# Decay terms and mLSTM query and key projections issued in a written order, with the convolution's evacuation cut into four parts

## The chip, the cores and the metric

The kernel runs on one core of one Trainium2 chip. Five engines work side by side, each through its own instructions in order: TensorE (PE) multiplies matrices into PSUM, VectorE (DVE), ScalarE (ACT) and GpSimd (POOL) work on elements, SyncE (SP) issues most of the transfers. The metric is device time in microseconds (us) of one execution; the median of the runs counts.

## The reference

One layer of a bidirectional encoder over 272 positions (16 learned meta tokens and 256 inputs), width 2048, all in float32. The stretch of the program that the change touches computes this:

```
u = rmsnorm(h, norm1_g)                       # (272, 2048)
proj = u @ w_in                               # one projection, columns split up
m_qk = proj[:, :2048]; m_gates = proj[:, 4096:4112]
qk = silu(dwconv_centred(m_qk, conv_w))       # width 3: x[t-1]*w0 + x[t]*w1 + x[t+1]*w2
q, k = qk[:, :1024], qk[:, 1024:]             # 4 heads x 256
li = gates of input, lf = log_sigmoid(gates of forgetting), forwards and backwards
# mLSTM: scores q.k weighted with exp(cumsum(lf) - ... + li - running maximum),
# forwards and backwards, divided by max(|den|, exp(-m)), normalised per head
```

Behind it come differential attention, the gated merge of both branches, the output projection and a ConvGLU. Nothing of these is changed.

## The kernel before

**Tiling.** Every projection is a `gemm` over blocks of 256 weight columns. The weights stream in *pieces* of 128 x 1024 numbers, four pieces to a block over 2048 rows. A piece lands in `raw` (a transfer by SP), ACT casts it to `hi` (L157) and DVE forms `lo` = raw - hi (L115); PE then runs hi x hi, hi x lo and lo x hi, 24 products of 128 x 258 (or 272) to a piece, into two accumulators `acc` of PSUM, one for each 128 columns. Pieces are split three ahead of their use (`prepare`, `weights`); four `hi` and `lo` buffers, six `raw` buffers and three `acc` buffers limit how far ahead anything can run. Two more tiles of PSUM hold pairs (`two`), one is single (`one`).

**Evacuation.** At a block's last piece `evac(ci, a)` runs for each of its two accumulators. For queries and keys it is that of `conv_silu`: DVE multiplies the accumulator with the norm `rQ` or `rB` (L161; this frees the accumulator), ACT applies the middle tap (L456), DVE adds the other two taps (L457, L459), ACT applies Silu (L151) and casts, DVE subtracts (L115). `later` is a list of functions that `gemm` calls once after the products of the next piece (`flush`).

**The opening.** The first query block and the gates' products run inside `with in_order()`, so their instructions keep the program's order on every engine. From them come the norm factors `ss` (Ln and Exp on ACT, L151), three diagonal tiles `dg` (L419), their products with ones (L428), the norm `rB` (a copy by ACT, L429), and the gate values `gsb` (a multiplication on DVE, L161, and a bias on ACT, L472).

**Decay terms.** `decay_terms` is a generator. It spreads `gsb` over partitions by eight small products (L483, L484; two tiles `two`), copies them out, forms log_sigmoid and runs scans and differences on DVE (L492 to L528) that fill `rows` and `acol`; two transposes (L533) end it. `weave(front, back)` takes one step of the generator `front`, then one piece of `back`, until `front` is done.

**What sets the order.** Outside `in_order()` a list scheduler of the framework picks, engine by engine, what stands next in each row of instructions; the engines keep to that row. Between the opening and the end of the program only activations are tied to each other: `activation` keeps functions of one table together, since a change of table costs an instruction of its own.

**Behind the stretch.** `values` projects the values while `heads1` makes the scores of four heads; then `heads2` (inside `weave` with the second branch's query projection `roped`) inverts the denominators, spreads them (`spread`), weighs the scores of a head (`merged`, into the single buffer `hl`), multiplies with the values (`outputs`: products `two<-hl`, then a square on ACT, L710, a cast, L711, and a subtraction on POOL, L712) and normalises (`normed`: products `one<-t` with ones).

Of the kernel before, what the change touches and what calls it, by code (L numbers as in the profile page):

```python
# [12 lines left out]
AF = mybir.ActivationFunctionType  # L13
# [51 lines left out]
def hybrid_layer(ctx, tc, x, meta, norm1_g, w_in, conv_w, gate_bias, mnorm_g, lq1, lk1, lq2, lk2,  # L65
# [23 lines left out]
    def unit(shape, dtype=F32):  # L89
        return units.tile([P] + shape, dtype, tag="u", name="u")  # L90
# [5 lines left out]
    def r1(n=NT, dtype=F32):  # L96
        return tmp.tile([P, n], dtype, tag="r1", name="r1")
# [16 lines left out]
    def low(out, src, hi):  # L114
        V.tensor_tensor(out=out, in0=src, in1=hi.bitcast(F32), op=ALU.subtract)  # L115

    @contextmanager
    def in_order():

        traced = nc.cur_bb.bb.instructions  # L120
        start, last = len(traced), {}
        yield
        for i in traced[start:]:
            if i.engine in last:
                behind(i, last[i.engine])
            last[i.engine] = i
# [8 lines left out]
    def activation(out, in_, func, **kw):  # L135

        k = KIND[func]
        if k != table[0]:
            before, since[:] = since[:], []
            table[0] = k  # L140
            if k == 0:
                first = S.preload_act_table_set("natural_log_exp_and_others").ins
                for i in before:
                    behind(first, i)
                before = [first]
                since.append(first)
            a = S.activation(out, in_, func, **kw)
            for j in before:
                behind(a.ins, j)
        else:  # L150
            a = S.activation(out, in_, func, **kw)  # L151
            behind(a.ins, since[0])
        since.append(a.ins)
        return a

    def split(hi, lo, src):
        S.copy(hi, src)  # L157
        low(lo, src, hi)

    def mul(o, a, b, eng=V):  # L160
        eng.tensor_tensor(out=o, in0=a, in1=b, op=ALU.mult)  # L161
# [98 lines left out]
    def weave(front, back):  # L260
        for _ in front:
            next(back, None)
        run(back)
# [184 lines left out]
    def conv_silu(dst, f, r, nt):  # L448
        hi, lo = pair(nt)
        dst.append((hi, lo))  # L450

        def evac(ci, a):
            j = f + ci
            u, c = r1(nt), r1(nt)
            mul(u, a, r)
            S.activation(c, u, AF.Copy, scale=cw(1, j))  # L456
            V.scalar_tensor_tensor(out=c[:, 1:nt], in0=u[:, 0:nt - 1], scalar=cw(0, j), in1=c[:, 1:nt],  # L457
                                   op0=ALU.mult, op1=ALU.add)
            V.scalar_tensor_tensor(out=c[:, 0:nt - 1], in0=u[:, 1:nt], scalar=cw(2, j), in1=c[:, 0:nt - 1],  # L459
                                   op0=ALU.mult, op1=ALU.add)  # L460
            activation(c, c, AF.Silu)
            split(hi[:, ci, :], lo[:, ci, :], c)
        return evac

    put = conv_silu(qs, 0, rQ, NT)
# [13 lines left out]
    def decay_terms():  # L479

        pli, plf = two(), two()
        for d in range(2):
            PE.matmul(pli[:, d, :L], sel[0:32, d * P:(d + 1) * P], gsb[0:32], start=True, stop=True)  # L483
            PE.matmul(plf[:, d, :L], sel[0:32, (2 + d) * P:(3 + d) * P], gsb[0:32], start=True, stop=True)  # L484
        li, lf, e, y, w = (unit([2, L]) for _ in range(5))
        S.copy(lf, plf[:, :, :L])
        S.copy(li, pli[:, :, :L])

        S.activation(e, lf, AF.Abs)
        activation(e, e, AF.Exp, scale=-1.0)  # L490
        yield
        V.tensor_scalar(out=y, in0=e, scalar1=1.0, scalar2=None, op0=ALU.add)  # L492
        V.tensor_scalar(out=w, in0=y, scalar1=1.0, scalar2=None, op0=ALU.subtract)
        V.tensor_tensor(out=e, in0=e, in1=w, op=ALU.subtract)
        activation(y, y, AF.Ln)
        activation(w, y, AF.Exp, scale=-1.0)
        yield
        mul(e, e, w)
        yield
        add(e, e, y)  # L500
        yield
        V.scalar_tensor_tensor(out=lf, in0=lf, scalar=0.0, in1=e, op0=ALU.min, op1=ALU.subtract)
        yield

        V.tensor_tensor_scan(out=m[:, 0, :], data0=lf[:, 0, :], data1=li[:, 0, :], initial=0.0, op0=ALU.add, op1=ALU.max)
        V.tensor_tensor_scan(out=m[:, 1, ::-1], data0=lf[:, 1, ::-1], data1=li[:, 1, ::-1], initial=0.0,
                             op0=ALU.add, op1=ALU.max)
        yield

        V.memset(rows[:, 258:260], 0.0)  # L510
        zero = unit([L])
        V.memset(zero, 0.0)
        acol = unit([2, L])
        for si, (s0, n) in enumerate(ST):
            cum = r1(L)
            V.tensor_tensor_scan(out=cum[:, s0:L], data0=lf[:, 0, s0:L], data1=zero[:, s0:L], initial=0.0,
                                 op0=ALU.add, op1=ALU.add)
            lo_t, at = max(s0, T0), (F0c, F1c, F2c)[si]
            V.tensor_tensor(out=rows[:, at:at + L - lo_t], in0=cum[:, lo_t:L], in1=m[:, 0, lo_t:L], op=ALU.subtract)
            V.tensor_tensor(out=acol[:, 0, s0:s0 + n], in0=li[:, 0, s0:s0 + n], in1=cum[:, s0:s0 + n], op=ALU.subtract)  # L520
            yield
            cum = r1(L)
            end, lo_c, at = s0 + n, min(s0, T0), (B0c, B1c, B2c)[si]
            rev = lambda a: a[:, lo_c:end][:, ::-1]
            V.tensor_tensor_scan(out=rev(cum), data0=rev(lf[:, 1, :]), data1=rev(zero), initial=0.0,
                                 op0=ALU.add, op1=ALU.add)
            V.tensor_tensor(out=rows[:, at:at + end - T0], in0=cum[:, T0:end], in1=m[:, 1, T0:end], op=ALU.subtract)
            V.tensor_tensor(out=acol[:, 1, s0:end], in0=li[:, 1, s0:end], in1=cum[:, s0:end], op=ALU.subtract)  # L528
            yield
        for d in range(2):  # L530
            pt = one()
            for si, (s0, n) in enumerate(ST):
                PE.transpose(pt[0:n, si * P:(si + 1) * P], acol[:, d, s0:s0 + n], ident)  # L533
            ptv = pt[:, 0:384].rearrange("p (s h q) -> p s h q", s=3, q=32)
            V.tensor_copy(aT[0:16, d, 0, :], ptv[0:16, 0, :, 0])
            V.tensor_copy(aT[:, d, 1:3, :], ptv[:, 1:3, :, 0])
            yield

    def keys():
        for b in range(4):  # L540
            yield from gemm(w_in, 16, K0 + 256 * b, 256, us, 0, L, conv_silu(ks, 8 + 2 * b, rB, L))

    def queries():
        for b in range(1, 4):
            yield from gemm(w_in, 16, Q0 + 256 * b, 256, us, T0, NT, conv_silu(qs, 2 * b, rQ, NT))

    weave(decay_terms(), chain(queries(), keys()))


    def values(c0, centred):  # L550
# [578 lines left out]
```

## Time and profile before

| | |
|---|---|
| median of 3 runs | 1569.02 us (1568.3 to 1572.68) |
| the profiled execution | 1567.98 us, of which the span of its instructions 1565.9 us |
| PE busy with products | 1542.8 us, 99% of the span |
| DVE, ACT, POOL busy | 66%, 49%, 5% |
| the chain that ended last | 95% PE, 2% DVE, 1% ACT |

PE's share is nearly the whole span, so the table says only that time lies where PE does not run, or runs at the lower of its two clocks; where that is, the rows below show.

### The profile page before, as it was taken

How to read it: one execution, taken by the hardware profiler on the slowest of the kernel's cores; microseconds unless marked ns; L12 is line 12 of the kernel's file. 1: busy time of each engine (PE TensorE's matmuls, PEld its weight loads, DVE VectorE, ACT ScalarE, POOL GpSimd, SP SyncE). 2: the span in 40 equal slices, each digit the busy share in tenths (PEclk: the TensorE clock that was granted, in tenths of full speed). 3: DMA queues.
4: the chain of work that ended last, by engine and by line, in shares of the span. 5: the costliest groups of instructions: out<-in, count | busy, mean ns of one | idle time of the engine just before them, and what ended most of it. 6: DMA issues, size and time to landing. Idle time of an engine off the chain costs nothing.

```text
span 1565.9 us, 28925 instructions
## 1 busy us (share of the span) xinstructions
PE 1542.8 (99%) x11825; PEld 1491.2 (95%) x11825; DVE 1028.8 (66%) x1617; ACT 763.7 (49%) x1147; POOL 81.0 (5%) x120
## 2 busy tenths in 40 slices
PE   8899989999999999999999999999999999999997
PEld 8899989999999999999999999999888999999887
DVE  6786688758886545665666676666444676766544
ACT  5656445444655433554555444444333454545443
POOL 1130113100000000000110000000000000000000
PEclk9999999999999999999999999999999999999999
DMA  9365425654456655555555555555555655655552
GB/s 262 108 202 161 149 82 166 188 167 131 124 174 201 188 177 188 185 180 182 195 167 182 187 183 188 181 183 178 198 189 188 188 176 188 187 179 186 184 193 95
DMA packets 255097, 274.52 MB, mean 175 GB/s; under 512 B 11460, under 2 KB 232773, under 8 KB 254949
## 3 DMA queue, kind: packets, MB, share of 16 engines
q1 hardware_dynamic: 251378, 269.01, 54.1%
q10 hardware_dynamic: 3587, 3.68, 0.8%
q8 instruction: 92, 1.51, 0.4%
q14 instruction: 40, 0.33, 0.1%
HBM read 270.55 MB, written 2.10 MB: 174 GB/s over the span
## 4 chain that ended last, share of the span: by engine, by line
PE 95%; DVE 2%; ACT 1%; issue 1%; POOL 0%; DMA 0%; SPq 0%; DVEq 0%; POOLq 0%; ACTq 0%
PE acc L172 90%; PE two L172 2%; DVE lo L115 1%; PE two L846 1%; PE one L172 0%; PE one L858 0%; PE two L568 0%; POOL t L712 0%; ACT hi L157 0%; PE two L977 0%; PE two L965 0%; DMA r<-in_norm_g_dram 0%; DVE u L730 0%; DVE u L115 0%; POOL t L164 0%
## 5 line engine op out<-in xcount | busy, mean ns | idle before, releaser
L172 PE MATMUL acc<-u,hi 128*128 128x258 f32 (+1 forms) x6592 | 1201.8, 285 | 4.9 <-DVE r L161 4.9
L172 PEld LDWEIGHTS acc<-u,hi 128*128 128x128 f32 x6592 | 1018.3, 189 | 7.2 <-DVE r L161 5.1
L172 PE MATMUL acc<-u,lo 128*128 128x258 f32 (+1 forms) x3296 | 924.0, 284 | 0.7 <-DVE lo L115 0.7
L115 DVE TENSOR_TENSOR lo<-raw,hi 128x1024 fp32r<-128x1024 f32 (+1 forms) x500 | 616.8, 1234 | 422.5 <-ACT hi L157 420.6
L157 ACT CAST hi<-raw 128x1024 fp32r<-128x1024 f32 (+1 forms) x500 | 523.3, 1048 | 648.4 <-PE acc L172 504.4
L172 PEld LDWEIGHTS acc<-u,lo 128*128 128x128 f32 x3296 | 621.3, 190 | 1.9 <-DVE lo L115 1.2
L172 PE MATMUL acc<-hi,u 128*128 128x512 f32 (+1 forms) x704 | 209.5, 381 | 0.0
L172 PEld LDWEIGHTS acc<-hi,u 128*128 128x128 f32 x704 | 130.6, 189 | 26.3
L172 PE MATMUL acc<-lo,u 128*128 128x512 f32 (+1 forms) x352 | 134.8, 383 | 0.0
L172 PEld LDWEIGHTS acc<-lo,u 128*128 128x128 f32 x352 | 66.2, 188 | 13.7
L161 DVE TENSOR_TENSOR r<-acc,r 128x258 f32<-128x258 f32 x88 | 37.3, 424 | 12.4 <-PE acc L172 12.4
L115 DVE TENSOR_TENSOR u<-r,u 128x256 fp32r<-128x256 f32 (+2 forms) x93 | 37.7, 436 | 4.9 <-ACT u L157 4.4
L1025 ACT ACTIVATE r<-r,fcT 128x256 f32<-128x256 f32 x88 | 39.9, 501 | 0.0
L157 ACT CAST u<-r 128x256 fp32r<-128x256 f32 (+2 forms) x93 | 34.6, 405 | 9.7 <-DVE r L161 7.0
L1026 DVE SCALAR_TENSOR_TENSOR r<-r,fcT,r 128x256 f32<-128x256 f32 x88 | 38.5, 479 | 0.0
L1027 DVE SCALAR_TENSOR_TENSOR r<-r,fcT,r 128x255 f32<-128x255 f32 x88 | 38.4, 479 | 0.0
L151 ACT ACTIVATE r<-r 128x256 f32<-128x256 f32 (+2 forms) x77 | 29.6, 412 | 3.5 <-DVE r L459 3.1
L161 DVE TENSOR_TENSOR r<-r,r 128x256 f32<-128x256 f32 (+1 forms) x57 | 22.1, 419 | 0.1
L161 DVE TENSOR_TENSOR r<-acc,u 128x258 f32<-128x258 f32 x32 | 13.5, 422 | 12.9 <-PE acc L172 12.9
L161 DVE TENSOR_TENSOR r<-acc,rB 128x272 f32<-128x272 f32 (+1 forms) x38 | 16.1, 429 | 4.8 <-PE acc L172 4.7
L164 DVE TENSOR_TENSOR u<-acc,u 128x512 f32<-128x512 f32 (+1 forms) x18 | 10.6, 625 | 12.7 <-PE acc L172 12.7
L151 ACT ACTIVATE t<-two,sm 128x272 f32<-128x272 f32 x32 | 15.3, 482 | 5.5 <-DVE sm L802 5.5
(241 smaller groups left out, 754.3 us busy)
## 6 DMA issues: line engine op xcount, KB each, us to landing
raw<-in_w_up_dram SPq DMA_DIRECT2D x176, 512.0 KB, 4.2
raw<-in_w_in_dram SPq DMA_DIRECT2D x175, 512.0 KB, 3.5
raw<-in_w_down_dram SPq DMA_DIRECT2D x88, 512.0 KB, 3.7
raw<-in_w_out_dram SPq DMA_DIRECT2D x32, 512.0 KB, 3.3
raw<-in_w_branch_m_dram SPq DMA_DIRECT2D x16, 512.0 KB, 3.3
raw<-in_w_branch_d_dram SPq DMA_DIRECT2D x16, 512.0 KB, 3.3
t<-in_x_dram ACTq DMA_DIRECT2D x8, 256.0 KB, 3.4
out_dram<-u SPq DMA_DIRECT2D x8, 256.0 KB, 2.8
```

The source lines that it names most:

```text
L115: V.tensor_tensor(out=out, in0=src, in1=hi.bitcast(F32), op=ALU.subtract)
L151: a = S.activation(out, in_, func, **kw)
L157: S.copy(hi, src)
L161: eng.tensor_tensor(out=o, in0=a, in1=b, op=ALU.mult)
L164: eng.tensor_tensor(out=o, in0=a, in1=b, op=ALU.add)
L172: PE.matmul(o, p, q, start=first and i == 0, stop=last and i == len(ops) - 1)
L846: PE.matmul(ps[:, i, 0:L], dq[h // 2][p][o:o + 64, h % 2, 2 + P * qt:2 + P * (qt + 1)], dk[h // 2][q][o:o + 64, h % 2, :], start=(p, q) == ...
L1025: S.activation(z, u[:, 2:NT], AF.Copy, scale=fcT[:, 1, f:f + 1])
L1026: V.scalar_tensor_tensor(out=z, in0=u[:, 1:NT - 1], scalar=fcT[:, 0, f:f + 1], in1=z, op0=ALU.mult, op1=ALU.add)
L1027: V.scalar_tensor_tensor(out=z[:, 0:SEQ - 1], in0=u[:, 3:NT], scalar=fcT[:, 2, f:f + 1], in1=z[:, 0:SEQ - 1], op0=ALU.mult, op1=ALU.add)
```

## The change

Two things change. `weave(decay_terms(), chain(queries(), keys()))` now stands inside `with in_order()`, so on each engine its instructions follow each other as the program writes them. And `evac` of `conv_silu` only multiplies the accumulators with the norm; the taps, Silu with its cast, and the subtraction follow in three functions that `later` calls after the first, second and third piece of the next block. `decay_terms` has three more yields, ahead of and behind its two copies out of PSUM.

```diff
--- before.py
+++ after.py
@@ -449,17 +449,33 @@
         hi, lo = pair(nt)
         dst.append((hi, lo))
 
+        uc = []
+
+        def taps():
+            for ci, (u, c) in enumerate(uc):
+                S.activation(c, u, AF.Copy, scale=cw(1, f + ci))
+            for ci, (u, c) in enumerate(uc):
+                V.scalar_tensor_tensor(out=c[:, 1:nt], in0=u[:, 0:nt - 1], scalar=cw(0, f + ci), in1=c[:, 1:nt],
+                                       op0=ALU.mult, op1=ALU.add)
+                V.scalar_tensor_tensor(out=c[:, 0:nt - 1], in0=u[:, 1:nt], scalar=cw(2, f + ci), in1=c[:, 0:nt - 1],
+                                       op0=ALU.mult, op1=ALU.add)
+            later.append(silu)
+
+        def silu():
+            for ci, (_, c) in enumerate(uc):
+                activation(c, c, AF.Silu)
+                S.copy(hi[:, ci, :], c)
+            later.append(rest)
+
+        def rest():
+            for ci, (_, c) in enumerate(uc):
+                low(lo[:, ci, :], c, hi[:, ci, :])
+
         def evac(ci, a):
-            j = f + ci
-            u, c = r1(nt), r1(nt)
-            mul(u, a, r)
-            S.activation(c, u, AF.Copy, scale=cw(1, j))
-            V.scalar_tensor_tensor(out=c[:, 1:nt], in0=u[:, 0:nt - 1], scalar=cw(0, j), in1=c[:, 1:nt],
-                                   op0=ALU.mult, op1=ALU.add)
-            V.scalar_tensor_tensor(out=c[:, 0:nt - 1], in0=u[:, 1:nt], scalar=cw(2, j), in1=c[:, 0:nt - 1],
-                                   op0=ALU.mult, op1=ALU.add)
-            activation(c, c, AF.Silu)
-            split(hi[:, ci, :], lo[:, ci, :], c)
+            uc.append((r1(nt), r1(nt)))
+            mul(uc[ci][0], a, r)
+            if ci == 1:
+                later.append(taps)
         return evac
 
     put = conv_silu(qs, 0, rQ, NT)
@@ -483,8 +499,11 @@
             PE.matmul(pli[:, d, :L], sel[0:32, d * P:(d + 1) * P], gsb[0:32], start=True, stop=True)
             PE.matmul(plf[:, d, :L], sel[0:32, (2 + d) * P:(3 + d) * P], gsb[0:32], start=True, stop=True)
         li, lf, e, y, w = (unit([2, L]) for _ in range(5))
+        yield
         S.copy(lf, plf[:, :, :L])
         S.copy(li, pli[:, :, :L])
+        yield
+        yield
 
         S.activation(e, lf, AF.Abs)
         activation(e, e, AF.Exp, scale=-1.0)
@@ -544,7 +563,8 @@
         for b in range(1, 4):
             yield from gemm(w_in, 16, Q0 + 256 * b, 256, us, T0, NT, conv_silu(qs, 2 * b, rQ, NT))
 
-    weave(decay_terms(), chain(queries(), keys()))
+    with in_order():
+        weave(decay_terms(), chain(queries(), keys()))
 
 
     def values(c0, centred):
```

Lines behind the change are numbered some 20 higher in it (L483 becomes L499, L457 becomes L458). The rows of instructions of the built programs differ from the opening to the end of `heads2`; behind that they are the same.

**PE, end of the opening.** `one<-r` are the products with the diagonal tiles (L428), L434 turns the parameters, L499 and L500 are the gates' products of `decay_terms`, `acc` the first streamed block. Rows of before have -, of the change +; those with a blank are in both.

```order
-L172 MATMUL acc<-u,lo 128x258
-L172 MATMUL acc<-u,hi 128x258
 L428 MATMUL one<-r_489,ones 128x16
 L428 MATMUL one<-r_490,ones 128x128
 L428 MATMUL one<-r_491,ones 128x128
+L434 MATMUL one<-ident,r_126 128x105
+L499 MATMUL two<-r_522,t_135 128x272
+L500 MATMUL two<-r_522,t_135 128x272
+L499 MATMUL two<-r_522,t_135 128x272
+L500 MATMUL two<-r_522,t_135 128x272
+L172 MATMUL acc<-u,hi 128x258 x2
+L172 MATMUL acc<-u,lo 128x258
```

Before, 73 streamed products stand between the last products of the opening and L428, and more ahead of the gates' products; now none does, and the first streamed product stands behind L500.

**DVE, the second streamed block's accumulators and the decay terms.** Before (`r_839` and `r_848` are the two products of an accumulator with the norm, L505 to L525 scans, L519 to L528 differences of the decay terms):

```order
L505 SCALAR_TENSOR_TENSOR u<-u 128x272
L506 SCALAR_TENSOR_TENSOR u<-u 128x272
L512 MEMSET u 128x272
L516 SCALAR_TENSOR_TENSOR r_771<-u 128x272
L525 SCALAR_TENSOR_TENSOR r_805<-u 128x16
L161 TENSOR_TENSOR r_839<-acc,rB 128x258
L519 TENSOR_TENSOR rows<-r_771,u 128x258
L520 TENSOR_TENSOR u<-u,r_771 128x16
L527 TENSOR_TENSOR rows<-r_805,u 128x2
L528 TENSOR_TENSOR u<-u,r_805 128x16
L161 TENSOR_TENSOR r_848<-acc,rB 128x258
```

In the change (`r_825` and `r_828` are the same two, L524 and L525 the first two scans):

```order
L521 SCALAR_TENSOR_TENSOR u<-u 128x544
L115 TENSOR_TENSOR lo<-raw,hi 128x1024
L161 TENSOR_TENSOR r_825<-acc,rB 128x258
L161 TENSOR_TENSOR r_828<-acc,rB 128x258
L524 SCALAR_TENSOR_TENSOR u<-u 128x272
L525 SCALAR_TENSOR_TENSOR u<-u 128x272
L115 TENSOR_TENSOR lo<-raw,hi 128x1024
L458 SCALAR_TENSOR_TENSOR r_826<-r_825,prmT,r_826 128x257
L460 SCALAR_TENSOR_TENSOR r_826<-r_825,prmT,r_826 128x257
L458 SCALAR_TENSOR_TENSOR r_829<-r_828,prmT,r_829 128x257
```

The two multiplications have moved ahead of the scans, and directly behind the split (`lo`) of a later piece.

**PE, heads 0 and 1 of `heads2`.** Before (`t_2598` and `t_2599` are the squares of head 0, `two<-hl` the products of head 1 that follow):

```order
L172 MATMUL acc<-u,lo 128x258
L172 MATMUL acc<-u,hi 128x258 x2
L172 MATMUL one<-t_2599,ones 128x258
L172 MATMUL one<-t_2598,ones 128x258
L172 MATMUL one<-t_2599,ones 128x258
L172 MATMUL acc<-u,lo 128x258
L172 MATMUL two<-hl,v_1597 128x258 x2
L172 MATMUL two<-hl,v_1598 128x258
L172 MATMUL two<-hl,u 128x258 x6
```

In the change (`t_2599` and `t_2600` are the squares of head 0, `t_2792` and `t_2793` those of head 1):

```order
L172 MATMUL two<-hl,u 128x258 x6
L172 MATMUL two<-hl,v_1585 128x258
L172 MATMUL one<-t_2599,ones 128x258
L172 MATMUL two<-hl,v_1585 128x258
L172 MATMUL two<-hl,v_1586 128x258
L172 MATMUL two<-hl,u 128x258 x6
L172 MATMUL two<-hl,v_1585 128x258 x2
L172 MATMUL two<-hl,v_1586 128x258
L172 MATMUL two<-hl,u 128x258 x6
L172 MATMUL one<-t_2600,ones 128x258
L172 MATMUL one<-t_2599,ones 128x258
L172 MATMUL one<-t_2792,ones 128x258
```

Before, 39 streamed products stand between the products of head 0 and the last ones on its squares, and the products of the two heads are apart; now the products of head 0, of head 1, and those on the squares of both heads stand next to each other without a streamed product.

## Rows read from the trace of the kernel before

**Rows 1.** Waits of PE over the whole span: total us, times, longest

```profile
PE acc L172 <- DVE r L161: 4.9, 1, 4.9
PE two L172 <- issue: 2.8, 1, 2.8
...
PE two L172 <- DVE u L723: 1.0, 1, 1.0
PE acc L172 <- DVE lo L115: 0.7, 2, 0.5
PE one L172 <- POOL t L712: 0.5, 1, 0.5
...
PE two L172 <- DVE u L115: 0.3, 1, 0.3
```

**Rows 2.** Timeline of PE, end of the opening: start us, us

```profile
27.95 4.14 PE L172 MATMUL two<-u 128*32 128x272 f32 x32
...
40.29 1.03 PE L428 MATMUL one<-r,ones 16*128 16x16 f32 x6
...
50.01 0.72 PE L483 MATMUL two<-r,t 32*128 32x272 f32 x2
...
52.04 0.39 PE L172 MATMUL acc<-u,lo 128*128 128x258 f32 x1
```

**Rows 3.** Timeline of ACT, the norm and the gate bias

```profile
35.32 0.30 ACT L151 ACTIVATE sm<-sm,eps 128x3 f32<-128x3 f32 x1 [1.47 <-DVE sm L415]
...
36.46 0.20 ACT L151 ACTIVATE sm<-sm 128x3 f32<-128x3 f32 x1
...
41.36 0.39 ACT L429 COPY rB<-one 128x272 f32<-128x272 f32 x1 [0.15 <-PE one L428]
...
46.76 0.52 ACT L472 ACTIVATE r<-r,gb 32x272 f32<-32x272 f32 x1 [0.88 <-DVE r L161]
```

**Rows 4.** Timeline of DVE, the norm and an accumulator's release

```profile
37.73 0.15 DVE L332 SCALAR_TENSOR_TENSOR sm<-sm 128x3 f32<-128x3 f32 x1
...
38.39 0.61 DVE L419 TENSOR_SCALAR r<-ident,sm 16x16 f32<-16x16 f32 x3
...
68.08 0.40 DVE L161 TENSOR_TENSOR r<-acc,rB 128x258 f32<-128x258 f32 x1
```

**Rows 5.** The chain that ended last: start us, us, what

```profile
68.54 5.00 PE acc L172 x23
...
491.58 231.18 PE acc L172 x1926
```

**Rows 6.** Stretches of 1 us: length, busy us of PE to POOL, granted clock, DMA

```profile
69.00:70.00 1.00, 1.00 (x7) 1.00 (x7) 1.00 (x4) 0.55 (x2) 0.00 (x0) 0.50 0.00 0
...
210.00:211.00 1.00, 1.00 (x7) 1.00 (x7) 1.00 (x6) 0.43 (x1) 0.57 (x1) 0.50 0.00 0
```

**Rows 7.** The page's costliest groups: a split; its mean in ns is second

```profile
L115 DVE TENSOR_TENSOR lo<-raw,hi 128x1024 fp32r<-128x1024 f32 (+1 forms) x500 | 616.8, 1234 | 422.5 <-ACT hi L157 420.6
```

**Rows 8.** Timeline of DVE beside POOL's broadcast of `rows`

```profile
75.67 2.18 DVE L115 TENSOR_TENSOR lo<-raw,hi 128x1024 fp32r<-128x1024 f32 x1
```

**Rows 9.** Timeline of POOL, the broadcast itself

```profile
74.30 6.07 POOL L606 PARTITION_BROADCAST FB<-rows  x4 [30.46 <-PE acc L172]
```

**Rows 10.** Timeline of PE: the last sums of `heads1`, the first `spread` of `heads2`

```profile
201.25 0.52 PE L172 MATMUL two<-t,selr 128*128 128x258 f32 x3
...
207.60 0.35 PE L172 MATMUL two<-u 128*128 128x258 f32 x1 [2.83 <-issue]
```

**Rows 11.** Timeline of ACT behind the products of head 0

```profile
219.83 0.60 ACT L710 ACTIVATE t<-two 128x516 f32<-128x516 f32 x1 [2.07 <-PE two L172]
220.46 0.62 ACT L711 CAST t<-t 128x516 fp32r<-128x516 f32 x1
220.99 0.84 ACT L157 CAST hl<-FB 128x774 fp32r<-128x774 f32 x1
```

**Rows 12.** Timeline of DVE and POOL behind the products of head 0

```profile
221.23 1.31 POOL L712 TENSOR_TENSOR t<-t,t 128x516 fp32r<-128x516 f32 x1 [10.65 <-ACT t L711]
222.71 0.96 DVE L115 TENSOR_TENSOR hl<-FB,hl 128x774 fp32r<-128x774 f32 x1
```

## The prediction

> **What bounds the kernel now.** The page comes first: PE is busy for 99% of the span and the chain that ended last lies on PE for 95%, so a change here counts by what PE waits for, or by the clock it runs at. The second view is the list of all that PE waited for [rows 1]: the reader is to see that one wait of 4.9 us stands out, for an accumulator that DVE had not released, and that four of 2.8, 1.0, 0.5 and 0.3 us (4.6 together) belong to one later place, `heads2`. A list of the same kind by stretches has nothing between these two places and nothing from there to the tail. The third view is the timeline of each engine at these places.
>
> A wait has a second price, which only the chain and the granted clock show. Behind the wait of 4.9 us, 23 streamed products take 5.00 us [rows 5]; at the rate of the long stretch (231.18 us for 1926, 0.120 us each [rows 5]) they would take 2.76. The granted clock there is 0.50 [rows 6], the lower level, 1.2 GHz. So this wait cost 4.9 + 2.2 = 7.1 us. The places in `heads2` also fell to 0.50 for a time [rows 6].
>
> **What the change does to the long wait.** Before, DVE's row holds the release of the second block's accumulators behind a chain of decay terms; the first release came at 68.08 [rows 4], and PE began at 68.54 [rows 5]. In the new row both releases stand ahead of the scans and need only what PE itself finishes. I count the whole 7.1 us as gone.
>
> **What the written order adds at the opening.** Before, PE fills the time in which the norm is worked out with 73 streamed products; now the gates' products must come first, and they need the norm. Step by step, from before's rows:
> - The opening's last 32 products began at 27.95 and took 4.14 us [rows 2]. The four streamed products ahead of them (0.5 us) are gone too, so PE is through at about 31.4.
> - Ln begins at 35.32 (0.30) and Exp takes 0.20 [rows 3]. Before, a cast and a split of the next pieces stood in between; the new rows of ACT and DVE don't hold them there, so Exp ends at 35.9. The three small DVE operations up to the diagonals take 0.66 (37.73 to 38.39 [rows 4]): the diagonals begin at 36.5 and end at 37.1. Nothing in the change can make PE's next product begin earlier.
> - The products with the diagonals take 1.03 [rows 2] and end near 37.6; the copy of `rB` (0.39 [rows 3]) ends at 38.0; three multiplications on DVE (0.40 for one [rows 4], which start 0.35 apart) end at 39.2; the gate bias (0.52 [rows 3]) ends at 39.7.
> - So the gates' products begin at 39.8, not 50.01 [rows 2], and the first streamed product comes behind them. They take 2.03 (50.01 to 52.04 [rows 2]), as before.
>
> Between 31.4 and 39.8 PE has 1.3 us of work (1.03 and one transpose): it waits 7.1 us. Since 4.9 us brought the clock down before, I take the same 2.2 us for the clock, and 0.4 for the products of the chain itself, which then run at half rate: 9.7 us. The bounds: 7.1 if the clock never falls, 12 if it stays down twice as long.
>
> What waits here on ACT and DVE costs nothing by itself: the first block's four pieces are split by then, and the fifth needs a buffer that PE frees.
>
> **What it adds in the query blocks.** DVE's work for a block is four splits of 1.23 [rows 7], two releases, four taps and two subtractions of about 0.4, some 7.7 us of the 11.5 us that PE takes for 96 products. The decay terms are 10.2 us of DVE, by my count of their rows at the spacing of the trace. Both stay the same, but before much of it ran while PE had 73 products to do; now it falls on four blocks: 4 x 7.7 + 10.2 = 41 of 46 us. DVE just keeps up, but any release that stands behind a split [the second excerpt of the change] comes late, since an accumulator is wanted half a piece after a block begins. I walked the rows: block by block, such waits come at the third query block (0.4 us), the first key block (0.8) and the second (1.3), where POOL's broadcast falls. Together 2.5; before, two waits for splits were 0.7 [rows 1], so +1.8. Bounds: 0, and 5 us, one split of 1.23 late in each of four blocks.
>
> The four parts of the evacuation bring no new work: the same operations in the same number. Two more table changes come, because the last key block's Silu now runs among the exponentials of `heads1`; ACT is free half of its time there, and the splits that queue behind them are wanted some 2 us later. I cost them at nothing; without that cover a late split would stop PE for what it is late, at most the 12 exponentials between them (an estimate, at the 0.4 us of other ACT rows of this size: some 5 us).
>
> **What it adds in `heads2`.** This is not written by the change; the scheduler placed it anew.
> - The reciprocal: from the end of the last sums (201.77) to the first `spread` (207.60) [rows 10] the chain takes 5.8 us. Before, 25 products (3.0 us) covered it and 2.8 were waited. Now 40 do (4.8): 1.0 is left. Behind it two short waits for splits, 0.8 together.
> - Heads 0 and 1: `hl` is one buffer, so head 1's products need head 0's to be through, then ACT's square and cast, and DVE's subtraction. In rows: the cast of `hl` begins 0.5 us behind the square's cast, and the new order has it directly behind the square, ending 1.5 us behind head 0's last product; DVE's part of 0.96 [rows 12] ends at 2.5. Head 1's products run to 4.6. Then its square (0.60 [rows 11]), another cast of `hl` (0.84), a Ln and its own cast (0.62) end near 6.9, and POOL's subtraction (1.31 [rows 12]) at 8.2. In these 8.2 us PE has 24 products (2.9 us): it waits 5.4, where before streamed products filled most of it.
>
> Together 1.0 + 0.8 + 5.4 = 7.2 against 4.6 [rows 1]: +2.6. The clock falls before and, I think, after; I take that as even. Bounds: -6 (no wait, no fall) and +6 (as counted, with another 2.2 for the clock, and POOL slower).
>
> **The sum.** 9.7 - 7.1 + 1.8 + 2.6 = +7.0 us. Against the profiled execution's own 1567.98 us (span 1565.9) that is 1575.0. The median of the runs, 1569.02, is 1.0 above this execution; the forecast for the median is 1576.
>
> **One rule beside a row.** While POOL broadcasts `rows` (6.07 us [rows 9]) a split takes 2.18 us [rows 8] instead of 1.23 [rows 7]: 0.95 more. In the change `rows` is complete some 10 us later, in the first key block, where DVE has no slack left. I carry 0.95 once, inside the 1.3. The Trainium skill, page "SBUF — State Buffer", section "Who interferes with whom", says that a DVE instruction with two SBUF inputs contends with a GpSimd instruction that reads SBUF, and that the second to issue is fully blocked for the whole instruction. The trace bears it out for single splits. By that rule all of the broadcast's 6.07 us may be lost to DVE.
>
> **Rivals.**
> 1. *DVE becomes the bound.* If the broadcast holds DVE for all its 6.07 us and not for one split's 0.95, the splits of the second key block are late by 5.1 more. For it: 41 of 46 us. Against it: before, the two splits beside the broadcast held PE only 0.7 us in all. PE would wait 5 us more: 1581. It decides when DVE's slack (5 us in four blocks) is used up ahead of the broadcast.
> 2. *Waits change places.* The written order's 9.7 replaces 7.1, the query blocks add nothing beyond the 0.7 of before, `heads2` comes out even: +2.6, 1571.5. For it: before's list shows no other wait in 100 us of key and value blocks. Against it: the rows of `heads2` in the change.
> 3. *Not slower.* `heads2` sets the sign. If head 1's chain is covered after all, because PE comes late to these rows and finds ACT, DVE and POOL done, then its 4.6 us and its clock loss of about 2 go, and the longer cover of the reciprocal does the rest: 9.7 - 7.1 + 1.8 - 6.6 = -2.2, 1567. It decides where the casts of `hl` and the squares end ahead of PE, some 5 us earlier than I count. Against it: they need PE's own products.
> 4. *Nothing changes.* The order of the rows could leave PE's waits as they are. The first excerpt speaks against that: no streamed product is ahead of L500.
>
> **Chances.** The forecast (1573.5 to 1579.5) 0.52, DVE bound (above that) 0.16, places changed (1569 to 1573.5) 0.20, not slower (below) 0.10, nothing 0.02. About 0.3%, 4.7 us, is what a measurement of this kernel tells from no change: slower means above 1573.7. So slower 0.68, within 0.3% 0.27, faster 0.05. The range that leaves out 2 in 10: 1568.5 to 1583.
>
> **What would show it.** Right: PE's list has a wait of about 5 us that ends with the products on the diagonals and one or two that end with the gates' products; the granted clock is 0.50 from there to about 45; the 4.9 us for DVE's release are gone; the second and third multiplication with `ones` in `heads2` have waits of 1 to 2 us behind ACT and POOL. Wrong: streamed products between 31 and 40 us; or a wait of more than 3 us for a split beside the broadcast; or no wait in `heads2` behind head 0.

## The result, and the profile after

The changed kernel takes 1579.62 us (median of four runs, 1579.08 to 1580.47), the kernel before 1569.12 (four runs): a ratio of 1.0070, 95% interval 1.0057 to 1.0082. It is 10.5 us slower, and the forecast of 1576.0 (1568.5 to 1583) with "slower" as the likeliest case was right. It lies 0.1 us above 1573.5 to 1579.5, the range that went with the forecast's own mechanism. The profiled execution took 1579.08 us, its span is 1577.3 (1565.9 before), the mean granted clock 0.992 (0.994 before).

First the list of PE's waits in the changed kernel, over the whole span, to be held against [rows 1]:

```profile
PE one L428 <- DVE r L419: 6.4, 1, 6.4
PE one L172 <- ACT u L780: 2.5, 1, 2.5
PE two L172 <- ACT hl L157: 1.9, 2, 1.4
...
PE acc L172 <- DVE r L161: 1.6, 3, 1.0
...
PE two L499 <- ACT r L488: 1.2, 1, 1.2
...
PE two L172 <- issue: 1.1, 1, 1.1
PE one L434 <- ACT rB L429: 0.5, 1, 0.5
PE one L172 <- POOL t L732: 0.5, 1, 0.5
PE one L552 <- DVE aT L555: 0.4, 1, 0.4
```

The wait of 4.9 us for DVE's release is gone; what is left for releases is 1.6 us in three places. In its stead stands one of 6.4 us in front of the products with the norm's diagonals (L428), and two more behind it on the same chain. The lines with `ACT u`, `ACT hl`, `issue` and `POOL t` belong to `heads2`.

PE's timeline at the end of the opening answers to [rows 2]:

```profile
27.31 4.14 PE L172 MATMUL two<-u 128*32 128x272 f32 x32
37.88 1.73 PE L428 MATMUL one<-r,ones 16*128 16x16 f32 x6 [6.42 <-DVE r L419]
40.08 0.44 PE L434 MATMUL one<-ident,r 105*128 105x105 f32 x1 [0.48 <-ACT rB L429]
41.76 1.27 PE L499 MATMUL two<-r,t 32*128 32x272 f32 x2 [1.25 <-ACT r L488]
...
45.68 0.80 PE L172 MATMUL acc<-u,hi 128*128 128x258 f32 x2
```

Between the opening's last 32 products and the first streamed one lie 14.2 us that hold only the chain of the norm and the gates' products. Before, 73 streamed products ran ahead of L428, and more ahead of the gates' products. The granted clock in stretches of 1 us (length, busy us of PE to POOL, clock, DMA) shows the second price:

```profile
36.00:37.00 1.00, 0.00 (x0) 0.00 (x0) 0.55 (x3) 0.50 (x2) 0.00 (x0) 0.50 1.11 349
...
48.00:49.00 1.00, 1.00 (x6) 1.00 (x6) 0.00 (x0) 0.96 (x4) 0.00 (x0) 0.50 0.00 0
49.00:50.00 1.00, 1.00 (x8) 1.00 (x7) 0.00 (x0) 0.81 (x3) 0.00 (x0) 0.71 0.00 0
```

The clock is at the lower level, 1.2 GHz, from 36 until beyond 49, though PE is busy without a break from 45.7 on. ACT's rows on that chain answer to [rows 3]:

```profile
36.28 0.30 ACT L151 ACTIVATE sm<-sm,eps 128x3 f32<-128x3 f32 x1 [1.92 <-DVE sm L415]
36.61 0.20 ACT L151 ACTIVATE sm<-sm 128x3 f32<-128x3 f32 x1
39.64 0.39 ACT L429 COPY rB<-one 128x272 f32<-128x272 f32 x1 [2.83 <-PE one L428]
41.19 0.52 ACT L488 ACTIVATE r<-r,gb 32x272 f32<-32x272 f32 x1 [1.16 <-DVE r L161]
```

Nothing stands between Ln and Exp any more, as forecast (0.33 us from one to the other, 1.14 before), but Ln itself begins at 36.28 and not at 35.32.

The chain that ended last has three rows of use (start, us, what); the second answers to [rows 5]:

```profile
45.75 13.45 PE acc L172 x96
...
500.99 231.34 PE acc L172 x1926
...
821.83 747.17 PE acc L172 x5356
```

The long stretch begins 9.4 us later than before (500.99 against 491.58) and runs at the same pace. So 9.4 of the 11.4 us by which the span is longer were lost ahead of it. The last row's counterpart in the kernel before, not shown above, is

```profile
812.25 745.33 PE acc L172 x5356
```

The same 5356 products, with no wait among them, took 1.8 us longer. That is most of the rest, and no step of the prediction has it.

### The profile page after: what moved, and what is told of

Read it like the earlier page. It is cut to its first block, busy times and chain, and to the rows that moved or that the text cites. A ratio compares the mean times of both kernels' runs of the same rounds, so it can differ in the third digit from the quotient of the medians.

```text
span 1577.3 us, 28921 instructions
## 1 busy us (share of the span) xinstructions
PE 1548.5 (98%) x11825; PEld 1495.6 (95%) x11825; DVE 1034.4 (66%) x1617; ACT 767.2 (49%) x1149; POOL 80.3 (5%) x120
## 4 chain that ended last, share of the span: by engine, by line
PE 95%; DVE 2%; ACT 1%; issue 1%; DMA 0%; POOL 0%; DVEq 0%; ACTq 0%
PE acc L172 90%; PE two L172 2%; DVE lo L115 1%; PE two L866 1%; PE one L172 0%; DMA raw<-in_w_in_dram 0%; PE one L878 0%; PE two L588 0%; ACT hi L157 0%; PE one L384 0%; DVE u L115 0%; PE two L997 0%; PE two L985 0%; DVE r L161 0%; DVE t L373 0%
## 5 line engine op out<-in xcount | busy, mean ns | idle before, releaser
L161 DVE TENSOR_TENSOR r<-acc,r 128x258 f32<-128x258 f32 x88 | 37.3, 424 | 13.3 <-PE acc L172 13.2
L157 ACT CAST u<-r 128x256 fp32r<-128x256 f32 (+1 forms) x77 | 28.0, 403 | 9.4 <-DVE r L161 7.0
L161 DVE TENSOR_TENSOR r<-acc,rB 128x272 f32<-128x272 f32 (+1 forms) x38 | 15.9, 430 | 9.9 <-PE acc L172 9.8
L161 DVE TENSOR_TENSOR r<-r,r 128x256 f32<-128x256 f32 (+1 forms) x57 | 22.1, 420 | 0.1
L161 DVE TENSOR_TENSOR r<-acc,u 128x258 f32<-128x258 f32 x32 | 13.5, 422 | 13.0 <-PE acc L172 13.0
L164 DVE TENSOR_TENSOR u<-acc,u 128x512 f32<-128x512 f32 (+1 forms) x18 | 10.6, 626 | 12.7 <-PE acc L172 12.7
```

The costliest lines, as they stand in the source:

```text
L164: eng.tensor_tensor(out=o, in0=a, in1=b, op=ALU.add)
```

## The experiments

Each ran beside the kernel before on the same chip; the ratios are to its runs there, whose medians were 1568.57 to 1569.53.

### 1 and 2. The two halves of the change, each alone

The first has the new `conv_silu` and the old `decay_terms` and `weave`; the second the reverse:

```diff
-    with in_order():
-        weave(decay_terms(), chain(queries(), keys()))
+    weave(decay_terms(), chain(queries(), keys()))
```

> The evacuation in four parts alone, with the decay terms and projections left in free order. My theory: the gain and the loss both come from the written order, not from the parts. The first release of the second block's accumulators still stands behind two scans in DVE's row, so a PE wait of 4 to 5 us for it stays near 64 to 69 us, with 2 us of low clock behind it; the opening has no PE wait over 1 us between 31 and 45. Time 1569 (1566 to 1572). Rival: it is the four parts that free the accumulators. Then the long wait falls under 2 us without the opening's loss, and the time is 1562 to 1564.

> The written order alone, with the evacuation in one part per accumulator. My theory: the opening loses the same 12 to 13 us as in the change (a wait of 6 to 7 us that ends with the products on the norm's diagonals, granted clock 0.50 behind it), and the second release of each block now stands on DVE behind the first one's convolution, Silu and subtraction, so PE waits 1 to 2 us at most of the query and key blocks: 1584 to 1592. Rival: the releases are early enough either way, the four parts change nothing: 1578 to 1581.

The four parts alone: 1570.65 us (11 runs), ratio 1.0013, interval 1.0004 to 1.0022. The order alone: 1596.45 (4 runs), 1.0177, 1.0163 to 1.0191. The first came as my theory had it in time, not quite in its rows: there is no wait at the opening, and the long wait is 3.0 us instead of 4 to 5, with a clock of 0.78 from 60 to 70. What it gained there went into `heads2`, whose waits in this kernel are those of the change (2.3, 1.9, 1.0, 0.5), and the last stretch of 5356 products takes 2.1 us more (747.39 against 745.33). So the four parts alone are enough to place `heads2` as it stands in the change. The written order alone changes `heads2` too, in another way (a wait of 5.8 us for the reciprocal, below).

The second was slower than even my theory said. PE's waits in the kernel with the order alone:

```profile
PE acc L172 <- ACT hi L157: 7.7, 3, 4.2
PE one L428 <- DVE r L419: 5.9, 1, 5.9
PE two L172 <- ACT u L157: 5.8, 1, 5.8
PE acc L172 <- DVE lo L115: 4.6, 5, 1.4
PE two L483 <- ACT r L472: 2.3, 1, 2.3
```

The opening's wait is there (second and fifth row). No row of the list names a release (`DVE r L161`): the 4.9 us are gone with the order alone. The rest is 12.3 us of waits for splits (casts `hi` and subtractions `lo`), which begin at 69, in the second query block, and end at 146, and a reciprocal in `heads2` (`u`, at 234) with nothing over it. That the splits are late because a whole evacuation now stands in front of them fits the places; it was not tried by itself. Of the 27.8 us that the order costs alone, the four parts give 16.8 back.

### 3. Streamed products ahead of the decay terms

```diff
     with in_order():
-        weave(decay_terms(), chain(queries(), keys()))
+        back = chain(queries(), keys())
+        held, later[:] = later[:], []
+        for _ in range(3):
+            next(back)
+        later += held
+        for _ in range(3):
+            next(back)
+        weave(decay_terms(), back)
```

> The change with six steps of the streamed query blocks ahead of the decay terms' first products in the written order (the first block's taps wait three of them). My theory: the opening's wait and its low clock go (12.8 us by the trace of the change against before), DVE's releases keep their early places so the 4.9 us wait does not come back, and the rest stays: 1567 (1565 to 1571), with granted clock 1.00 from 31 to 60. Rival: DVE becomes the bound, since the decay terms' 10 us now fall on fewer blocks; then waits of 4 us or more for splits or releases come in the key blocks, and the time is 1571 to 1576.

It takes 1568.07 us (11 runs, 1566.12 to 1570.49), ratio 0.9994, interval 0.9986 to 1.0003: 11.5 us less than the change and in my theory's range. Of the 11.5, 4.0 lie in the last stretch of 5356 products (743.19 us against 747.17 in the change), which the edit does not touch. From 34 to 60 the clock is 1.00 and L428 waits for nothing. But four streamed products had been placed ahead of the opening's last 32 and waited 2.5 us for their weights, at 28.86:

```profile
28.86 0.51 PE L172 MATMUL acc<-u,hi 128*128 128x258 f32 x2 [2.50 <-ACT hi L157]
```

The clock was at 0.50 behind it from 30 to 33, and a release at 50.56 was 1.9 us late, behind the first block's taps.

### 4. The same, mended

The written order now begins behind the opening's last product on PE (`opened`; the edit that lets `in_order` take it is left out here), the taps wait four steps and the decay terms come after five. Against experiment 3:

```diff
-    with in_order():
+    with in_order(opened):
...
-        for _ in range(3):
+        for _ in range(4):
             next(back)
         later += held
-        for _ in range(3):
+        for _ in range(1):
             next(back)
```

> As the late start before it, with two mends: the streamed products of the written order may not stand ahead of the opening's last 32 products, and the first block's taps wait four steps, so that the first release is not behind them; the decay terms' products follow after five steps. My theory: the opening's 12.8 us go whole, the 4.9 us wait does not come back, the key blocks keep 2 to 4 us of waits, and heads2 stays as in the change: 1566 (1563 to 1569), the pace of the long later stages leaving 3 us either way. Granted clock 1.00 from 31 to 60. Rival: DVE is the bound of these blocks, and what the opening gives back comes again as waits of 5 us or more for splits and releases between 45 and 110: 1571 to 1576.

It takes 1567.47 us (11 runs), ratio 0.9994, 0.9986 to 1.0003, 12.2 less than the change: my theory. Both mended waits are gone; in the blocks up to 110 PE waits 2.4 us in all, 1.3 the longest, and the clock never leaves 1.00 there. The rival is out: DVE has room for the decay terms in these blocks. That the kernel is still no faster than before lies mainly in `heads2`, whose waits are those of the change (2.3, 1.9, 1.1, 0.4).

### 5 and 6. The wait and the clock apart

The first fills the wait for the norm with 28 products of ones into an accumulator that nothing reads; the second has three more behind L428 and seven behind L434, in a written order with them (shown is the first):

```diff
+        idle = acc()
+        for _ in range(28):
+            PE.matmul(idle, onesr, onesr[:, 0:1].to_broadcast([P, 512]), start=True, stop=True)
```

> The change with 28 products of ones (128x512, into an accumulator that nothing reads) behind the opening's last products, so that TensorE is busy while the norm is worked out; the wait for the norm itself stays. My theory: of the 12.8 us that the opening lost, 8.2 are waits and 4.6 are the lower clock behind them; the granted clock stays 1.00 from 31 to 50, and the time falls by 4 to 5: 1575 (1574 to 1576.5). Rival: the clock falls with the two later waits of 0.5 and 1.25 us anyway, or the fillers only push the diagonals' products back: 1579 to 1581.

> The fillers again, with three more products of ones behind the norm's diagonals and seven behind the transpose, so that TensorE has work in the two later waits too (they add nothing to the output). My theory: the granted clock stays 1.00 from 31 to 50, and only the waits for the norm stay (about 8 us); the time is 4 to 4.5 less than the change: 1575.3 (1574 to 1577). Rival: what the first fillers gave back (2.1 us in their profiled execution, nothing in the median) is scatter, and keeping the clock up gives nothing that can be measured: 1578.5 to 1580.5.

The first takes 1579.73 us (5 runs, from 1577.02 to 1582.01), ratio 1.0071, 1.0057 to 1.0085. That is the rival's range, and the trace shows the rival's reason: the clock is 1.00 up to 43.0, then falls all the same, behind waits of 0.47 and 1.37 us (rows below). But the execution that was profiled took 1577.53 and the runs lie 5.0 us apart, so this median does not price the clock.

```profile
42.00:43.00 1.00, 1.00 (x6) 0.60 (x5) 0.96 (x3) 0.16 (x1) 0.00 (x0) 0.98 0.00 0
43.00:44.00 1.00, 1.00 (x6) 1.00 (x6) 0.02 (x1) 0.98 (x3) 0.00 (x0) 0.50 0.03 8
...
46.00:47.00 1.00, 1.00 (x9) 1.00 (x9) 0.00 (x0) 0.87 (x3) 0.00 (x0) 0.82 0.00 0
```

The second takes 1576.45 (5 runs, 1575.96 to 1578.92), ratio 1.0052, 1.0038 to 1.0065. Its clock is 1.00 from 30 to 50, and it is 3.2 us faster than the change though the norm comes no earlier (Ln begins at 36.34). That is my theory, with 3.2 for the 4 to 4.5 expected. So of the opening's loss about a quarter is clock by the medians; by the rows it is a third (below).

### 7, 8 and 9. `heads2` in a written order

The change, and then the version of experiment 4, with `heads2` in a written order, the rotation's evacuation of the query blocks in three parts, and streamed key blocks behind (the evacuation and two moved yields are left out here):

```diff
-    weave(heads2(), roped(dq, DQ0, T0, NT))
-    run(roped(dk, DK0, 0, L))
+    back = chain(roped(dq, DQ0, T0, NT), roped(dk, DK0, 0, L))
+    with in_order():
+        for _ in heads2():
+            next(back)
+    run(back)
```

> The change with heads2 and the differential query projection in a written order too (four steps of streamed products for each head, the rotation's evacuation in three parts, streamed key blocks behind it so that they do not run out). My theory: heads2's loss in the change is 9.4 us of waits and low clock by the spacing of its products, and nearly all of it is a matter of order: 2 to 3 us stay, the time is 1573 (1571 to 1575.5). Rival: DVE is busy 52 of 60 us there, so the waits come back for splits: 1577 to 1582.

> Both of these together. My theory: the gains add, since they lie 150 us apart: about 13 less than the change from the opening and about 6 from heads2, so 1560 (1556 to 1564). Rival: one of them is taken back by waits of DVE, 1566 or more.

On the change: 1589.3 us (4 runs), ratio 1.0131, 1.0118 to 1.0145. With the mended opening: 1575.87 (5 runs), 1.0045, 1.0031 to 1.0058. My theory fell; the first time is above the rival's range too, the second in it. The opening's gain is there (13.4 between the two), but `heads2` lost 8 to 10 us where 6 were to be won. In the second of them PE waits in front of the first `spread`:

```profile
194.57 1.70 PE L172 MATMUL two<-u 128*128 128x258 f32 x4 [5.53 <-ACT u L157]
```

The two streamed steps that I had meant to cover the reciprocal were placed ahead of the last sums, since those stood outside the written order; behind the sums nothing was left. The third version puts two steps ahead of the sums and holds two behind them:

```diff
+    for _ in range(2):
+        next(back)
-    with in_order():
+    with in_order(*summed):
```

> Both written orders, with heads2's first rows mended: two steps of the differential queries stand ahead of the last sums and two behind them, so that 48 products cover the reciprocal. My theory: the 5.5 us wait for the reciprocal and about 2.5 of low clock go, the seven waits of 4.2 for splits stay: 1567.5 (1565.5 to 1570). Rival: the cover moves the sums back and the chain starts as much later, so that half of the wait stays: 1571 to 1574.

It takes 1573.4 us (6 runs), ratio 1.0030, 1.0018 to 1.0041: in the rival's range, but not by its reason. The wait for the reciprocal is gone whole, and the seven waits for splits (4.2 us), which were to stay, are down to two of 1.0 in all. But a new wait is in their place, for ACT's copy of the query accumulators, which now stands in ACT's written row behind casts that wait for a head:

```profile
PE acc L172 <- ACT u L804: 7.3, 3, 3.2
```

### 10. The same order on TensorE alone

```diff
-    with in_order(*summed):
+    with in_order(*summed, only=summed[0].engine):
```

> The same with the order of heads2 written for TensorE alone; the other engines' rows there are left to the scheduler. My theory: the splits come ahead of work that nothing waits for yet, so part of the 4.2 us of waits for them goes as well: 1565 (1562 to 1568). Rival: DVE is simply full in that stretch, and the rows' order on it does not matter: the same as the run beside it within 1.5 us.

It takes 1563.82 us (5 runs, 1563.09 to 1564.72), ratio 0.9967, interval 0.9954 to 0.9979: faster than the kernel before by 5 us, than the change by 16. My theory holds in time, though what went was ACT's 7.3 us and not the waits for splits. PE's order is the same, row by row, up to 277 (behind `heads2` some streamed products change places); ACT, DVE and POOL have theirs from the scheduler. From 220 to 280 PE waits for nothing:

```profile
220.00:240.00 20.00, 20.00 (x169) 20.00 (x168) 19.49 (x34) 10.22 (x15) 5.77 (x4) 1.00 0.47 135
240.00:260.00 20.00, 20.00 (x165) 20.00 (x164) 16.79 (x25) 11.23 (x17) 7.37 (x5) 1.00 0.51 141
```

DVE is busy 19.5 of 20 us in the first of these stretches and does not hold PE up.

### 11. The change with TensorE's row left free

The other way round, at the opening: the written order on all engines but TensorE.

> The change with its written order kept on every engine but TensorE, whose row is left to the scheduler. My theory: the opening's loss belongs to TensorE's row alone, so streamed products fill the wait for the norm again; DVE's early releases stay, and the 4.9 us wait does not come back: no wait over 2 us between 28 and 60, and 1568 (1566 to 1571). Rival: the other engines' written rows hold up the splits and releases that those streamed products need, so that the wait only moves some us back: a wait of 4 us or more between 38 and 70, 1573 to 1579.

It takes 1576.74 us (5 runs), ratio 1.0049, 1.0035 to 1.0063: the rival. The scheduler does put streamed products ahead of L428 again, which waits for nothing. But the fifth streamed piece is now late, and PE waits up to 51.91:

```profile
51.91 0.80 PE L174 MATMUL acc<-u,hi 128*128 128x258 f32 x2 [4.77 <-ACT hi L159]
```

ACT's rows ahead of it, in the same kernel, are the decay terms' copy out of `two`, a table load, Silu with its casts (left out here), and then the cast that PE wants:

```profile
47.36 0.62 ACT L507 COPY u<-two 128x544 f32<-128x544 f32 x1
48.00 1.28 ACT L149 ACT_TABLE_LOAD   x1
...
50.81 1.04 ACT L159 CAST hi<-raw 128x1024 fp32r<-128x1024 f32 x1
```

So the opening's loss belongs to the sequence in which the code is written, decay terms first, and not to TensorE's row alone: another engine that keeps the sequence, here ACT, can bring back a part of it.

### 12. The change once more

> The change itself once more, for the pace of the streamed products in the stages that the change does not touch: 120.3 ns from one to the next between 880 and 1080, where the kernel before had 119.6. My theory: the pace belongs to the program, so it is 120.2 to 120.4 again, and the 2 us by which the change is late beyond its waits stand in every execution: 1579 to 1580.5. Rival: it belongs to the execution, and any value from 119.3 to 120.5 comes.

It takes 1579.86 us (2 runs), ratio 1.0071, 1.0052 to 1.0089, and the last stretch of its chain reads

```profile
822.79 747.17 PE acc L172 x5356
```

the same 747.17 as in the first execution of the change. My theory: the pace belongs to the program, as far as one repetition shows.

## Why the prediction was right, step by step

**The long wait, 7.1 us gone.** Right. No release is waited for longer than 1.0, and the clock is 1.00 there. Experiment 1 shows that the four parts alone take off only 1.9 of the 4.9. Experiment 2 has no wait for a release either, so the order alone is enough for this; without the four parts PE waits 12.3 us for splits instead.

**The opening, 9.7 us.** The mechanism, the place and the order of the waits are as written; the size was too small, and just above the upper bound of 12. In the trace of the change it is 12.7: waits of 6.42, 0.48 and 1.25 (8.15, not 7.1), and 4.5 us of low clock (not 2.6): 0.7 in L428 (1.73 against 1.03 [rows 2]), 1.9 in the gates' products (41.76 to 45.68 against 2.03 [rows 2]), and 1.9 in the 96 streamed products behind (13.45 for the 11.5 that they take at 0.120). Two numbers were off. I began the norm's chain at Ln's old time, 35.32, and it came 1.0 later: the piece that DVE splits ahead of the last squares was ready half a microsecond later, and the reduction began 0.54 us behind the end of DVE's last square, 0.10 before; what held it there stays open. And the term for the products of the chain itself was too small: I had 0.4 for them and kept the gates' products at 2.03, but the clock was at 0.50 from the first of them to the last, and they lost 2.6 (0.7 and 1.9). The streamed products lost 1.9, near the 2.2 that I took from [rows 5]. Experiment 6 puts the clock's part at 3.2 by medians, between 2.6 and 4.5. Experiments 3 and 4 are 11.5 and 12.2 us faster than the change, but 4.0 and 1.1 of that lie in the last stretch and both have waits of their own, so they show that the opening's loss goes and not its size.

**The query and key blocks, +1.8.** Waits of 0.96, 0.36, 0.37 and 0.24 us stand in PE's timeline between 73 and 99 where 0.7 stood before: +1.2. The third query block and the two key blocks are the places named; their sizes (0.96, 0.36 and 0.61, where I had 0.4, 0.8 and 1.3) fit in sum better than one by one. The two additional table loads cost nothing: there is no wait for ACT in the blocks that follow.

**`heads2`, +2.6.** The waits are 1.07 for the reciprocal, 0.48, 1.42, 2.54 and 0.45 (5.96, forecast 7.2, before 4.6). The chain of heads 0 and 1 runs as I counted it. Behind the end of head 0's last product (229.41) the cast of `hl` ends at 1.4 us (forecast 1.5), DVE's part at 2.4 (2.5), head 1's products at 4.7 (4.6), ACT's last cast at 7.0 (6.9) and POOL's subtraction at 8.4 (8.2); PE waits 4.4 us in it, where I had 5.4. Of the multiplications with `ones`, for which I had 1 to 2 us at two places, one waits 2.54 and the next 0.45. Adding up what PE's products there take beyond the median for their width, waits and low clock together, gives 9.7 against 7.5 before (from 200 to 265): +2.2. The longest wait has a link that I did not name. It is booked to ACT, but the rows of DVE show another end:

```profile
235.52 0.96 DVE L115 TENSOR_TENSOR hl<-FB,hl 128x774 fp32r<-128x774 f32 x1 [3.74 <-ACT hl L157]
235.75 0.62 ACT L731 CAST t<-t 128x516 fp32r<-128x516 f32 x1
236.40 0.48 DVE L331 TENSOR_SCALAR r<-one,eps 128x258 f32<-128x258 f32 x1
236.51 1.27 POOL L732 TENSOR_TENSOR t<-t,t 128x516 fp32r<-128x516 f32 x1 [3.58 <-issue]
...
237.03 0.35 PE L172 MATMUL one<-t,ones 128*128 128x258 f32 x1 [2.54 <-ACT u L780]
237.84 1.01 PE L172 MATMUL one<-t,ones 128*128 128x258 f32 x3 [0.45 <-POOL t L732]
```

`one` is a single buffer, head 0's variance in it is read at L331, and that reading stands in DVE's row behind the subtraction for `hl`, which waits for ACT. PE begins 0.15 us after L331 has ended. That this is the cause was read from the rows, not tried alone. It moves little: the cast that this product needs ends only at 236.37 (L731), and the next product waits for POOL's subtraction until 237.78 in any case.

**The sum.** 12.7 - 7.1 + 1.2 + 2.2 = 9.0, forecast 7.0; the long stretch begins 9.4 late. With 1.8 for the slower pace of the last stretch, which I had not in the sum at all, it is 10.8 of the 11.4 us between the spans. The forecast was 3.6 us low in the median; by the terms it is 3.0 from the opening and 1.8 from the pace, less 1.0 that I had given too much to the query blocks and `heads2`. Without the pace, which no step foresaw, the time would lie inside 1573.5 to 1579.5; as it is, it lies just above, in the part that I had given to a bound on DVE, which did not come.

**The rivals.** DVE did not become the bound, and I had misread the broadcast: the `x4` in [rows 9] counts four instructions, and I took them for one. In the change they run from 92.77 for 7.05 us and take turns with DVE's operations. These are rows of both engines' timelines, from stretches that hold one broadcast each:

```profile
92.77 2.34 POOL L626 PARTITION_BROADCAST FB<-rows  x1 [51.19 <-issue]
93.81 1.40 DVE L115 TENSOR_TENSOR u<-r,u 128x258 fp32r<-128x258 f32 x1
94.97 1.43 POOL L626 PARTITION_BROADCAST FB<-rows  x1
95.13 1.38 DVE L115 TENSOR_TENSOR u<-r,u 128x258 fp32r<-128x258 f32 x1
96.25 1.46 POOL L626 PARTITION_BROADCAST FB<-rows  x1
96.58 2.04 DVE L115 TENSOR_TENSOR lo<-raw,hi 128x1024 fp32r<-128x1024 f32 x1
97.55 2.26 POOL L626 PARTITION_BROADCAST FB<-rows  x1
```

```profile
81.81 0.76 DVE L115 TENSOR_TENSOR u<-r,u 128x258 fp32r<-128x258 f32 x2
```

The first subtraction ends 0.1 us behind the first broadcast (95.21 and 95.11), the second as much behind the second (96.51 and 96.40). The last broadcast ends 1.2 behind the split that began ahead of it (99.81 and 98.62) and is 0.8 longer than the one before it. So each DVE operation is held for about one broadcast, not for all four. The pair of subtractions took 2.71 where the pair at 81.81 took 0.76, and the split 2.04 where 1.22 is usual: DVE lost 2.8 us, more than the 0.95 that I carried, and PE waited 0.4 and 0.2 for it. Before, four operations beside the broadcasts (from 74.53 to 81.27, the split of [rows 8] among them) had lost some 3.6 us in the same way, so this cost was no new one.

The Trainium skill, page "SBUF — State Buffer", section "Summary: rules for kernel authors", says that where a DVE instruction has two SBUF inputs and a GpSimd instruction reads SBUF, the second to issue is fully blocked until the first has finished. The trace agrees, with the 0.1 us above, for one instruction at a time.

"Not slower" by a covered `heads2` did not come; experiment 10 shows that the cover can be had, there by an order that was written for it.

## What to carry to other kernels

A written order takes from the scheduler the products with which it would have filled a wait, so write first what waits for nothing, and the chain that waits (here the norm's) behind as many streamed products as it lasts. Write it for the engine whose waits decide and leave the others free: in `heads2` the same rows of TensorE cost 1573.4 us with all engines written and 1563.82 with TensorE alone. And cost the lower clock by all the work that runs while it is down: here the products between the waits lost 2.6 us and the streamed ones behind them 1.9.

## What the runs showed of the hardware that was not expected

The 5356 products of the last stretch, in which PE waits for nothing and the granted clock is 1.00, took 747.17 us in five runs of four programs: the change, its repetition, both with fillers and the one with TensorE's row free, whose rows stand in a different order. In the other programs it went from 743.19 (experiment 3) over 745.33 (before), 746.08 (experiment 4) and 747.39 (four parts alone) to 748.74 (order alone). The four programs ask for their buffers in nearly the same sequence (the fillers take one accumulator more), so operands may lie in the same places; whether that is the cause was not tried. It is worth up to 5.5 us between kernels that do the same work, as much as some of the effects measured here.

In experiment 5 the clock fell to 0.50 at 43 though the wait of 6 us had been filled, and the runs of this kernel lie 5.0 us apart, those of the second filler 3.0 and of the change 1.4. Why they scatter stays open.
